# Four latent value blocks projected between the first head's scores, with weight preparation spread differently

## The chip, the cores and the metric

One core of a Trainium2 chip runs the whole program. It has a matrix engine (TensorE, "PE" in the profile, with its weight loads as "PEld"), a vector engine (VectorE, DVE), a scalar engine (ScalarE, ACT), a general engine (GpSimd, POOL) and a queue engine that issues transfers (SyncE, SP). Each engine runs its own instructions in its own order, and semaphores hold an instruction until what it needs is there. The metric is device time of one execution in microseconds (us). Times inside an execution come from one profiled execution and count from its span's start.

## The reference, cut to what matters

The program is one step of a two-layer diffusion backbone on 640 tokens: 512 latent tokens and 128 prompt tokens, width 1024. Layer 0 has two kinds of attention side by side, eight heads each, and one output projection over both:

```python
a_mla = attend_blocked(q, concat([k_lat, k_ctx]), concat([v_lat, v_ctx]), MLA_SCALE)   # 8 latent heads
a_na  = neighbourhood_attention(nq, nk, nv, c_nk, c_nv, rpb)                           # 8 neighbourhood heads
return concat([a_mla, a_na]) @ w_out
```

In the latent attention, keys and values are expanded from a 256-wide compressed latent: `kv = ckv @ w_ukv`, for 512 latent tokens, 128 cached tokens and 128 prompt tokens. The change lies where the neighbourhood heads end and the latent heads begin. Layer 1 has grouped-query attention, and every layer ends in a SwiGLU feed-forward network ("FFN"). Before each sub-layer a modulation (shift, scale, gate) is worked out from the conditioning: `silu(cond) @ w_mod + b_mod`.

## The kernel before, in words

**Precision.** A matrix operand is kept as two parts, a high part (a rounded copy) and a low part (the rest), and a product is three matmuls: high by high, high by low, low by high (`mm3`). So every operand costs one copy by ACT and one subtraction by DVE or POOL. `unit` (L168) does this for a slab of weights: load into a raw buffer, high part on ACT (L173), low part on DVE or POOL (L174). `rsplit` (L472) does it for a finished 128x640 activation, `pt_split` (L395, rows L401 and L402) for a transposed block of probabilities, and `vsplit` (L467, rows L469 and L470) for a projected block of values. Slabs sit in a ring of three raw buffers and a ring of three weight buffers, so that a slab can only be prepared once an older one is no longer read.

**Neighbourhood heads, then latent heads.** The loop over `h` from 0 to 7 in the first stage runs neighbourhood heads (names begin with n: `ns` scores, `np` probabilities, `nt` their transposes, `nts` the split transposes, `no` the head's output, `npp3` the prompt pair of heads 6 and 7). While head 7 runs, the keys (`mk`, `kT`) and queries (`mq`) of latent head 0 are projected too, from weights `wm0`; `mla_w(p)` makes `wm0` to `wm3`, the key and query weights of latent head pairs, and `wmv` holds the weights of the values. The next stage has latent heads 0 to 7 (names begin with m: `ms` scores, `mn` row maximum, `mp` probabilities from ACT at L992, `mr` the reciprocal sums, `mt` transposes, `mts` split transposes, `mo` the output). Each latent head has four score pieces s0 to s3, two query pieces q0 and q1 for the next head, and, of the head before, transposes and value products.

**Values.** The values of all latent heads are six blocks `mv0` to `mv5` of 128 tokens each; one block is six matmuls of 128x512. In the kernel before, mv0 and mv1 are projected (`mv_early`) among the last neighbourhood head's work and left in two banks of the matrix engine's result memory (PSUM), of the kind "y". After that stage is closed, `k_set` prepares keys of the odd heads (`kTo`, `kTq`), `vsplit` takes mv0 and mv1 out of their banks, and `open_y(s=2)` replaces the four "y" banks by two pairs of kind "s". The score pieces alternate between these two pairs, so the first score piece of latent head 0 writes where mv0 and mv1 lay. Blocks mv2 to mv5 are projected behind that by `mv_late`, in banks of another kind ("m"), one after the other, ahead of the first score.

**Order.** The order of pieces on TensorE is written out: `sequence(order, pieces)` runs the pieces by name, each bound behind the last matmul of the one before (`issue_after`). `MLA_ORDER[0]` and `MLA_ORDER[1]` are the orders of even and odd latent heads, and names of pieces that a head does not have are skipped. On the other engines a scheduler in the framework sets the order, so that a small edit can move rows there. `after(inst, fn)` holds work back until a named instruction has been placed, and `exps[h, j]` is the exponential of piece j of latent head h.

**Side work of the FFN.** While the FFN of layer 0 runs, DVE works out modulation columns of layer 1 from tiles of weights (`wm`, rows `junk`, two of 1.22 us for a tile). `mod_side` gets a plan with a number of tiles for each step of the FFN: steps "fb" over blocks of the hidden width, then steps "n" over the output blocks.

Of the kernel before, what the change touches and what calls it, by code (L numbers as in the profile page):

```python
# [14 lines left out]
ALU = mybir.AluOpType  # L15
# [36 lines left out]
def body(ctx, tc, xT, vecs, crow, wm0, wm0g1, wm0g, wm1, wA, wNV, wNA, wMK, wMV, wOA, wGQ, wGK, wGV, wOC,  # L52
# [112 lines left out]
        nc.sync.dma_start(raw[:, :n], src)  # L165
        return raw[:, :n]

    def unit(src, n, name, lo="v", pool=None, bufs=3):  # L168

        raw = load(src, n, name + "r")  # L170
        t = (pool or wp).tile([P, 2, 1024], F32R, tag="w", bufs=bufs, name=name)
        hi, lw = t[:, 0, :n], t[:, 1, :n]
        S.activation(hi, raw, AF.Copy)  # L173
        (V if lo == "v" else G).tensor_tensor(lw, raw, f(hi), ALU.subtract)  # L174
        return hi, lw

# [292 lines left out]
        S.activation(dst[:, :, 0:64], s3, AF.Copy)  # L469
        V.tensor_tensor(dst[:, :, 64:128], s3, f(dst[:, :, 0:64]), ALU.subtract)  # L470

    def rsplit(src, name):  # L472
        h = ring.tile([P, T], F32R, tag="hh", name=name + "h")
        l = ring.tile([P, T], F32R, tag="hl", name=name + "l")
        S.activation(h, src, AF.Copy)
        V.tensor_tensor(l, src, f(h), ALU.subtract)
# [350 lines left out]

    def mla_w(p):
        if p not in wmk:
            wmk[p] = unit(wMK[p], 768, f"wm{p}", lo="g")  # L830
        return wmk[p]

    def latents():
# [72 lines left out]
    for h in range(8):  # L906
        p, r = divmod(h, 2)
        if r == 0:
            oN.append(ring.tile([P, T], F32, tag="x", name=f"oN{p}"))
            pfirst, psecond = prompt_pair([nv[4][:, 2 * p + i, :] for i in range(2)], oN[p], ab, f"npp{p}",  # L910
                                         lambda name: bank(name, "y"))
        pts = []
        sc = na_scores(h, bm, pts)
        if h < 7:
            bm = na_bias(h + 1)
        qh, ql, ks = [t[r] for t in nqk[p]]
        pieces = named("s", sc)

        def prompt_scores(pss, qh=qh, ql=ql, ks=ks):
            PE.matmul(pss, qh[:, NS:T], ks[:, 896:1024], start=True, stop=False)  # L920
            PE.matmul(pss, ql[:, NS:T], ks[:, 896:1024], start=False, stop=True)
        pieces["sp"] = pfirst(r, prompt_scores)
        if p < 3:
            pieces.update(named("q", na_q(p + 1) if r == 0 else na_k(p + 1)))
        for n, at in enumerate(M_AT):
            if h == at:
                pieces.update(named("n" if "m0" in pieces else "m", mod0(4 + n, lambda n=n: bank(f"mod{4 + n}", "y"),
                                                                               mod_raw_w if h == 6 else mod_raw)))
        if h == 7:
            pieces.update(k_pieces(0, ybank))  # L930
            pieces.update(named("u", q_pieces(0, ybank, lambda c: ring.tile([P, T], F32R, tag="h" + c, name=f"mq{c}0"),
                                              lazy(lambda: load(tabM[:, 0, :], T, "tq0")))))
        sequence(NA_ORDER[h] if h else "q0 q1 s0 m0 q2 s1 sp q3 q4 q5 m1 q6 q7 m2", {**pieces, **tail})
        tail = na_values(h, pts, oN[p])
        if r == 1:
            tail.update(psecond)
        if h == 6:
            lat = latents()
            kT = [[ring.tile([P, T], F32R, tag="h" + c, name=f"kT{c}{r}") for r in range(2)] for c in "hl"]
            kTp = ring.tile([P, T], F32R, tag="x", name="kTp")  # L940
            even_keys, first_odd = [[(kT[i][r], kTp[:, P * (2 * i + r):P * (2 * i + r + 1)]) for i in range(2)] for r in range(2)]
            odd_keys = [first_odd]
            cqs = [rsplit(cq[u], f"cqs{u}") for u in range(2)]
            mla_w(0)
            wmv = unit(wMV, 1024, "wmv")
        if h == 7:
            for r in range(2):
                k_set(r, (slice(64, 128), slice(0, 64))[r], (0, 1, 2), kr)
# [75 lines left out]

    def mv_late(i):
        vsplit(mv[i], mv_of(i, bank))
    BESIDE = ()
    for i in range(6):
        if i not in mvb and i not in BESIDE:
            mv_late(i)  # L1030
# [5 lines left out]
    for h in range(8):  # L1036
# [22 lines left out]
        if r == 1:  # L1059
            tail.update(psecond)  # L1060
        if h in (0, 2, 4):
            oNs.append(after(exps[h, 3], lambda: rsplit(oN[len(oNs)], f"oNs{len(oNs)}")))
    oNs.append(after(exps[7, 2], lambda: rsplit(oN[3], "oNs3")))
    oMs = [after(exps[7, 3], lambda: rsplit(oM[p], f"oMs{p}")) for p in range(3)]
    sequence("w3 t0 y3 w4 t1 y4 t2 v0 t3 l0 pt v1 t4 l1 v2 v3 l2 v4 l3 l4 pv", {**tail, **late})
# [638 lines left out]
    def x_again(n):  # L1704
# [5 lines left out]
    op = ffn_open(0)  # L1710
    box, nxt = next_mod("h01", gs[0][1], mods[0], SH2, op[7])
    side, before = mod_side([(0, wm0g, G2)] + [(1, wm1[j:j + 8], j) for j in (SH1, SC1, G1, SH2, SC2)],
                            lambda kind, i: int(i > 4 and i % 3 > 0 or i == 21) if kind == "fb" else
                            (0, 1, 1, 1, 2, 2, 2, 2, 3, 3, 3, 3, 3, 2, 2, 2)[i])
    x, pend = mixer_out(wOA, oMs + oNs, [4, 5, 6, 7, 0, 1, 2, 3], x_again, mods[0], "oa", nxt, op[-1], before(op[1], op[5], (1, 1, 1, 1, 0, 0, 0)), True)
    box2, nxt = next_mod("h10", gs[1][0], mods[1], SH1)
    x, pend = ffn(0, x, pend, box["m"], nxt, side, op)
# [379 lines left out]
```

## Time and profile before

| what | value |
|---|---|
| time, median of three runs | 1475.41 us (1473.70 to 1478.78) |
| the profiled execution | 1473.37 us, span 1471.5 us, mean granted clock of TensorE 0.997 |
| PE busy | 1439.2 us (98%) |
| DVE busy | 1235.1 us (84%) |
| ACT busy | 783.9 us (53%) |
| POOL busy | 173.9 us (12%) |
| chain that ended last, by engine | PE 86%, DVE 6%, ACT 4% |

How to read it: the profiled execution is 2.04 us faster than the median of the runs, and 1.87 us of its time lie outside its span. PE's busy share is an average; what a change in one stage is worth shows in that stage's own idle time. A row of the timeline has its start, its duration, the engine, the line, the operation, what it writes and reads, the shape, how many instructions it groups, and in square brackets the idle time ahead of it with the instruction that ended it. A row of a window has, for each engine, the busy time and count of instructions in that stretch, then TensorE's granted clock, the share of the transfer engines and GB/s.

### The profile page before, as it was taken

To read this page: it belongs to the slowest core of one execution; us is meant where nothing else is said; L and a number is where in the kernel's file an instruction comes from. 1 tells how busy PE (TensorE), PEld (TensorE's weight loads), DVE (VectorE), ACT (ScalarE), POOL (GpSimd) and SP (SyncE) were. 2 spreads that over 40 slices of the span, in tenths; PEclk is the share of its full clock that TensorE was granted. 3 is DMA by queue.
4 is the path that set the end of the run, shared out by engine and by line. 5 is a ranking of instruction groups with operands and counts; after the bars stand their busy time and mean duration, and the time that the engine had idled before them with its cause. 6 is when DMAs were issued, how large, how long until landed. Compare 5 with 4: busy or idle time off the path is not lost.

```text
span 1471.5 us, 25831 instructions
## 1 busy us (share of the span) xinstructions
PE 1439.2 (98%) x9764; PEld 1388.8 (94%) x9764; DVE 1235.1 (84%) x2391; ACT 783.9 (53%) x1539; POOL 173.9 (12%) x270
## 2 busy tenths in 40 slices
PE   5999999999999999999999999999999999999997
PEld 3989978889999999999999999989999999999997
DVE  5877798877998888965997888888899898989976
ACT  5446687763755555531223656672656555555443
POOL 0046645420000000000000122220000000000000
PEclk9999999999999999999999999999999999999999
DMA  9653431025165555569764310115245555548572
GB/s 372 212 161 125 145 115 44 15 89 184 48 213 165 169 168 170 181 233 321 235 223 150 97 33 30 45 44 185 87 167 187 179 177 182 177 143 296 184 270 72
DMA packets 79636, 231.48 MB, mean 157 GB/s; under 512 B 8856, under 2 KB 13240, under 8 KB 79128
## 3 DMA queue, kind: packets, MB, share of 16 engines
q1 hardware_dynamic: 77152, 225.43, 45.7%
q10 hardware_dynamic: 1944, 3.48, 0.7%
q8 instruction: 76, 1.25, 0.3%
q0 software_dynamic: 416, 0.93, 0.2%
q14 instruction: 48, 0.39, 0.1%
HBM read 193.15 MB, written 36.66 MB: 156 GB/s over the span
## 4 chain that ended last, share of the span: by engine, by line
PE 86%; DVE 6%; ACT 4%; issue 2%; DMA 2%; POOL 1%; DVEq 0%; ACTq 0%; POOLq 0%
PE fg L64 21%; PE fd L64 9%; PE fgo L64 5%; PE fo L64 5%; PE fu L64 4%; PE gq L64 3%; PE fdo L64 2%; PE gs L64 2%; PE go L64 2%; PE fuo L64 1%; PE nq L64 1%; PE gt L68 1%; PE nk L64 1%; PE gvp L64 1%; PE mod L64 1%
## 5 line engine op out<-in xcount | busy, mean ns | idle before, releaser
L1664 DVE SCALAR_TENSOR_TENSOR junk<-wm,cb 128x1024 bf16<-128x1024 f32 x88 | 107.2, 1218 | 6.4 <-DMA wm<-in_wm 5.5
L64 PE MATMUL gq<-h10h,wgq 128*128 128x320 f32 x256 | 65.8, 316 | 0.0
L267 POOL TENSOR_SCALAR h10h<-h10t,gs,mods 128x320 fp32r<-128x320 f32 x4 | 3.9, 990 | 429.4 <-DVE h10t L261 427.1
L1404 ACT ACTIVATE wY<-s 128x1024 fp32r<-128x1024 f32 x38 | 40.3, 1061 | 25.4 <-PE fg L64 21.4
L1932 POOL TENSOR_TENSOR xr<-xw,fn1rs 128x320 f32<-128x320 f32 x2 | 1.7, 862 | 412.8 <-ACT fn1rs L235 412.8
L1404 ACT ACTIVATE wZ<-s 128x1024 fp32r<-128x1024 f32 x38 | 40.1, 1056 | 16.0 <-PE fd L64 11.7
L1405 DVE TENSOR_TENSOR wZ<-s,wZ 128x1024 fp32r<-128x1024 f32 x38 | 46.3, 1219 | 1.6
L1405 DVE TENSOR_TENSOR wY<-s,wY 128x1024 fp32r<-128x1024 f32 x38 | 46.3, 1219 | 0.3
L64 PEld LDWEIGHTS gq<-h10h,wgq 128*128 128x128 f32 x256 | 44.9, 189 | 0.6
L1513 DVE TENSOR_TENSOR sg<-up,sg 128x640 f32<-128x640 f32 x38 | 31.2, 822 | 15.8 <-ACT sg L1512 15.0
L1512 ACT ACTIVATE sg<-fg 128x320 f32<-128x320 f32 x38 | 16.7, 438 | 48.4 <-PE fg L64 48.4
L1534 ACT ACTIVATE p<-fd 128x320 f32<-128x320 f32 x38 | 16.6, 438 | 44.1 <-PE fd L64 44.1
L64 PE MATMUL gq<-h10l,wgq 128*128 128x320 f32 x128 | 39.4, 308 | 0.0
L1869 ACT ACTIVATE gp<-gs,gb,rq 128x640 f32<-128x640 f32 (+1 forms) x40 | 31.8, 796 | 13.2 <-DVE gb L1868 11.8
L64 PE MATMUL fg<-h01E,wW 128*128 128x320 f32 x228 | 36.6, 309 | 0.5 <-DVE g L1544 0.5
L64 PE MATMUL fg<-h11N,wZ 128*128 128x320 f32 x228 | 36.7, 309 | 0.0
L64 PE MATMUL fg<-h01q,wX 128*128 128x320 f32 x228 | 36.7, 309 | 0.0
L64 PE MATMUL fu<-h11q,wX 128*128 128x320 f32 x228 | 36.6, 309 | 0.0
L64 PE MATMUL fd<-h11q,wZ 128*128 128x320 f32 x228 | 36.6, 309 | 0.0
L64 PE MATMUL fd<-h01q,wZ 128*128 128x320 f32 x228 | 36.5, 309 | 0.0
L64 PE MATMUL fg<-h01C,wY 128*128 128x320 f32 x228 | 36.5, 309 | 0.0
L64 PE MATMUL fg<-h11q,wX 128*128 128x320 f32 x228 | 36.5, 309 | 0.0
(3421 smaller groups left out, 5299.4 us busy)
## 6 DMA issues: line engine op xcount, KB each, us to landing
wm<-in_wm SPq DMA_DIRECT2D x48, 512.0 KB, 4.2
mraw<-in_wm SPq DMA_DIRECT2D x8, 1024.0 KB, 13.1
mraw<-in_wm SPq DMA_DIRECT2D x14, 512.0 KB, 4.1
wmv<-in_wm0g SPq DMA_DIRECT2D x8, 512.0 KB, 4.1
wm<-in_wm0g SPq DMA_DIRECT2D x8, 512.0 KB, 5.1
ruo<-in_wFO SPq DMA_DIRECT2D x8, 512.0 KB, 3.9
rgo<-in_wFO SPq DMA_DIRECT2D x8, 512.0 KB, 5.3
x<-in_xT SPq DMA_DIRECT2D x8, 320.0 KB, 5.4
```

What stands on the lines that cost most here:

```text
L64: cls.last = nc.tensor.matmul(*a, **k)
L68: cls.last = nc.tensor.transpose(*a, **k)
L267: G.tensor_scalar(h[:, c0:c1], t, self.gsl[:, k, 0:1], self.ml[:, self.sh + k, 0:1], ALU.mult, ALU.add)
L1404: S.activation(h, src, AF.Copy)
L1405: V.tensor_tensor(w_, src, f(h), ALU.subtract)
L1512: last = S.activation(sg[:, 0:HT], g[:, :HT], AF.Silu, scale=-1.0)
L1513: V.tensor_tensor(sg, up, sg, ALU.mult)
L1534: S.activation(p5, b5[:, :HT], AF.Copy)
L1664: V.scalar_tensor_tensor(junk, raw, 1.0, cb[:, c, :], ALU.mult, ALU.mult, accum_out=mods[l][:, j0 + i, c:c + 1])
L1869: gexp[h, j] = S.activation(dst, src, AF.Exp, bias=nb, scale=rq[:, j:j + 1], accum_out=ll[:, j:j + 1])
L1932: G.tensor_tensor(x[k][:, c0:c1], root[1][k], nrm.rs[:, c0:c1], ALU.mult)
```

## The change

There are five edits.

1. The high part of the value weights `wmv` is made by POOL (`hi_by=G`), no longer by ACT.
2. `mla_w(p)` for p = 1, 2, 3 is held until the exponential of piece 1 of latent head 2p-2: `wm1` is prepared in head 0, `wm2` in head 2 and `wm3` in head 4. Before, all three were prepared as soon as a buffer was free.
3. Value blocks 2 to 5 are not projected ahead of the first score but inside latent head 0, whose order is now written out as s0 q0 s1 b2 q1 b3 s2 b4 s3 b5 (b2 is block 2).
4. The split of the finished neighbourhood outputs (`oNs0` to `oNs2`, in latent heads 0, 2 and 4) is done in two halves of 320 columns.
5. In the side plan of layer 0's FFN, one tile goes from "fb" step 20 to "n" step 0.

```diff
-    def unit(src, n, name, lo="v", pool=None, bufs=3):
+    def unit(src, n, name, lo="v", pool=None, bufs=3, hi_by=None):
...
-        S.activation(hi, raw, AF.Copy)
+        if hi_by:
+            hi_by.tensor_scalar(hi, raw, 1.0, 0.0, ALU.mult, ALU.add)
+        else:
+            S.activation(hi, raw, AF.Copy)
...
-    def rsplit(src, name):
+    def rsplit(src, name, parts=((0, T),)):
         h = ring.tile([P, T], F32R, tag="hh", name=name + "h")
         l = ring.tile([P, T], F32R, tag="hl", name=name + "l")
-        S.activation(h, src, AF.Copy)
-        V.tensor_tensor(l, src, f(h), ALU.subtract)
+        for c0, c1 in parts:
+            S.activation(h[:, c0:c1], src[:, c0:c1], AF.Copy)
+            V.tensor_tensor(l[:, c0:c1], src[:, c0:c1], f(h[:, c0:c1]), ALU.subtract)
         return h, l
...
-            wmk[p] = unit(wMK[p], 768, f"wm{p}", lo="g")
+            wmk[p] = after(exps.get((2 * p - 2, 1)), lambda: unit(wMK[p], 768, f"wm{p}", lo="g"))
...
-            wmv = unit(wMV, 1024, "wmv")
+            wmv = unit(wMV, 1024, "wmv", hi_by=G)
...
-    BESIDE = ()
+    BESIDE = 2, 3, 4, 5
...
-        sequence(MLA_ORDER[r], {**pieces, **late, **{k: v for k, v in tail.items() if k not in ("v3", "v4", "l3", "l4")}})
+        sequence(MLA_ORDER[r] if h else "s0 q0 s1 b2 q1 b3 s2 b4 s3 b5", {**pieces, **late, **{k: v for k, v in tail.items() if k not in ("v3", "v4", "l3", "l4")}})
...
-            oNs.append(after(exps[h, 3], lambda: rsplit(oN[len(oNs)], f"oNs{len(oNs)}")))
+            oNs.append(after(exps[h, 3], lambda: rsplit(oN[len(oNs)], f"oNs{len(oNs)}", HALF)))
...
-                            lambda kind, i: int(i > 4 and i % 3 > 0 or i == 21) if kind == "fb" else
-                            (0, 1, 1, 1, 2, 2, 2, 2, 3, 3, 3, 3, 3, 2, 2, 2)[i])
+                            lambda kind, i: int(4 < i < 20 and i % 3 > 0 or i == 21) if kind == "fb" else
+                            (1, 1, 1, 1, 2, 2, 2, 2, 3, 3, 3, 3, 3, 2, 2, 2)[i])
```

**TensorE, from the last neighbourhood work to the first latent score.** `npp3o` is the last product of the neighbourhood heads, `mv5` the last value block, `ms0_0` the first score piece and `mq10` the first query piece. Before, 16 rows (24 matmuls) of mv2 to mv5 follow `npp3o`; the last four of them and what follows:

```order
L64 MATMUL mv5_2858<-wmv_2560,ckph_2524 128x512 x2
L64 MATMUL mv5_2858<-wmv_2560,ckpl_2525 128x512
L64 MATMUL mv5_2858<-wmv_2560,ckph_2524 128x512 x2
L64 MATMUL mv5_2858<-wmv_2560,ckpl_2525 128x512
L64 MATMUL ms0_0_2872<-kTh0_2540,mqh0_2565 128x320 x2
L64 MATMUL ms0_0_2872<-kTl0_2542,mqh0_2565 128x320 x2
L64 MATMUL ms0_0_2872<-kTh0_2540,mql0_2566 128x320 x2
L64 MATMUL mq10_2886<-cqs0h_2545,wm0_2555 128x320
```

With the change:

```order
L64 MATMUL npp3o_2792<-npp3pth_2757,nv4_775 128x128
L64 MATMUL npp3o_2792<-npp3ptl_2758,nv4_775 128x128
L64 MATMUL ms0_0_2836<-kTh0_2540,mqh0_2565 128x320 x2
L64 MATMUL ms0_0_2836<-kTl0_2542,mqh0_2565 128x320 x2
L64 MATMUL ms0_0_2836<-kTh0_2540,mql0_2566 128x320 x2
L64 MATMUL mq10_2850<-cqs0h_2545,wm0_2555 128x320
```

The first score now stands directly behind `npp3o`; the 24 matmuls of mv2 to mv5 stand between the later pieces of head 0.

**DVE, the same stretch.** `oN3` takes the last neighbourhood outputs, `kTol` and `kTql` are odd keys, `mv` the value blocks, `mn0_0` the maximum of the first score piece. Before:

```order
L462 TENSOR_TENSOR oN3_2366<-npp3o_2792,npp3h_2797 64x128 x2
L867 TENSOR_TENSOR kTol_2815<-kr_587,kToh_2813 64x512
L867 TENSOR_TENSOR kTol_2815<-kr_587,kToh_2813 64x128
L867 TENSOR_TENSOR kTql_2816<-kr_587,kTqh_2814 64x128
L470 TENSOR_TENSOR mv0_2807<-mv0_2761,mv0_2807 128x8x64
L470 TENSOR_TENSOR mv1_2808<-mv1_2768,mv1_2808 128x8x64
L470 TENSOR_TENSOR mv2_2809<-mv2_2831,mv2_2809 128x8x64
L470 TENSOR_TENSOR mv3_2810<-mv3_2840,mv3_2810 128x8x64
```

With the change:

```order
L465 TENSOR_TENSOR oN3_2366<-npp3o_2792,npp3h_2797 64x128 x2
L871 TENSOR_TENSOR kTol_2815<-kr_587,kToh_2813 64x512
L871 TENSOR_TENSOR kTol_2815<-kr_587,kToh_2813 64x128
L871 TENSOR_TENSOR kTql_2816<-kr_587,kTqh_2814 64x128
L473 TENSOR_TENSOR mv0_2807<-mv0_2761,mv0_2807 128x8x64
L473 TENSOR_TENSOR mv1_2808<-mv1_2768,mv1_2808 128x8x64
L994 TENSOR_REDUCE mn0_0_2843<-ms0_0_2836 128x1
L893 TENSOR_TENSOR mqt10_2857<-mq10_2850,tq_2805 128x320
```

Up to mv1's low part the order is the same. The first score piece waits for that row in both programs, because it writes the banks that mv1 is read from.

**ACT, latent head 4.** `mts3_1h` to `mts3_4h` are split transposes of head 3, `mp4_2` a probability piece of head 4, `oaw0` and `oaw1` weights of the output projection. Before:

```order
L401 ACTIVATE mts3_1h_3560<-mt3_1_3555 128x512
L440 ACTIVATE mpp2p_3490,mpp2l0_3576<-ms4_2_3564,mpp2m0_3574 128x128
L401 ACTIVATE mts3_2h_3595<-mt3_2_3590 128x512
L173 ACTIVATE oaw1_4305<-oaw1r_4303 128x1024
L992 ACTIVATE mp4_2_3583,ml4_3491<-ms4_2_3564,mn4_2_3581 128x640
L890 ACTIVATE mqh5_3492<-mqt51_3607 128x320
L401 ACTIVATE mts3_3h_3617<-mt3_3_3612 128x512
```

With the change:

```order
L404 ACTIVATE mts3_1h_3564<-mt3_1_3559 128x512
L176 ACTIVATE wm3_3686<-wm3r_3684 128x768
L443 ACTIVATE mpp2p_3494,mpp2l0_3580<-ms4_2_3568,mpp2m0_3578 128x128
L404 ACTIVATE mts3_2h_3599<-mt3_2_3594 128x512
L176 ACTIVATE oaw0_4264<-oaw0r_4262 128x1024
L996 ACTIVATE mp4_2_3587,ml4_3495<-ms4_2_3568,mn4_2_3585 128x640
L894 ACTIVATE mqh5_3496<-mqt51_3611 128x320
L404 ACTIVATE mts3_3h_3621<-mt3_3_3616 128x512
L176 ACTIVATE oaw1_4311<-oaw1r_4309 128x1024
```

`wm3` and `oaw0` now stand in head 4 ahead of `oaw1`. Before, `wm3` stood in head 0 and `oaw0` in head 2. On DVE the low parts of `oaw0` and `oaw1` move in the same way.

## The prediction

> **What bounds the kernel now.** The page's busy shares come first, then TensorE's (PE) list of waits.
>
> ```profile
> PE 1439.2 (98%) x9764; PEld 1388.8 (94%) x9764; DVE 1235.1 (84%) x2391; ACT 783.9 (53%) x1539; POOL 173.9 (12%) x270
> ```
>
> ```profile
> PE ms L64 <- ACT mp L992: 2.6, 4, 1.0
> PE mo L64 <- DVE mts_0l L402: 1.1, 2, 0.9
> ```
>
> PE sets the time, and an edit is worth what it does to PE's idle time. The windows over the changed stage (PE first, with its busy time and count, then PEld, DVE, ACT, POOL, the granted clock) show where idle time is left:
>
> ```profile
> 200.00:225.00 25.00, 21.94 (x131) 19.11 (x130) 22.09 (x59) 18.69 (x46) 8.36 (x10) 1.00 0.25 79
> 225.00:250.00 25.00, 23.94 (x161) 21.91 (x160) 19.82 (x46) 20.04 (x48) 15.52 (x19) 1.00 0.14 44
> 250.00:275.00 25.00, 24.75 (x163) 22.11 (x162) 22.86 (x49) 20.20 (x49) 10.85 (x14) 1.00 0.07 22
> 275.00:300.00 25.00, 23.84 (x157) 21.31 (x156) 22.14 (x48) 19.55 (x47) 10.76 (x14) 1.00 0.07 22
> 300.00:325.00 25.00, 23.63 (x152) 20.46 (x152) 20.62 (x39) 17.45 (x37) 7.79 (x8) 1.00 0.19 64
> 600.00:625.00 25.00, 25.00 (x173) 25.00 (x172) 23.65 (x37) 13.19 (x21) 0.00 (x0) 1.00 0.59 185
> ```
>
> From 200 to 325 PE is idle for 3.06 + 1.06 + 0.25 + 1.16 + 1.37 = 6.90 us: all that this stage can give. In the FFN (last row) it is never idle. PE's timeline has the places:
>
> ```profile
> 203.39 0.50 PE L64 MATMUL no<-nts_0l,nv 128*128 128x512 f32 x1 [1.61 <-DVE nts_0l L402]
> 205.35 0.39 PE L64 MATMUL mk<-ckph,wm 128*128 128x256 f32 x1 [0.86 <-DVE nm L784]
> 215.59 0.28 PE L64 MATMUL npp3o<-npp3ptl,nv 128*128 128x128 f32 x1
> 215.70 0.67 PE L64 MATMUL mv<-wmv,ckh 128*128 128x512 f32 x2
> 221.23 0.45 PE L64 MATMUL ms<-kTh,mqh 128*128 128x320 f32 x2
> 224.51 0.56 PE L64 MATMUL ms<-kTh,mqh 128*128 128x320 f32 x2 [0.49 <-ACT mp L992]
> 228.71 0.56 PE L64 MATMUL ms<-kTh,mqh 128*128 128x320 f32 x2 [0.97 <-ACT mp L992]
> 278.77 0.56 PE L64 MATMUL ms<-kTh,mqh 128*128 128x320 f32 x2 [0.16 <-ACT mp L992]
> 285.08 0.49 PE L64 MATMUL mo<-mts_0h,mv 128*128 128x512 f32 x1 [0.89 <-DVE mts_0l L402]
> ```
>
> **Edit 1 and wm1's hold: upstream gain, -0.75.** ACT loses two operations:
>
> ```profile
> 197.47 1.05 ACT L173 ACTIVATE wmv<-wmvr 128x1024 fp32r<-128x1024 f32 x1
> 199.62 0.85 ACT L173 ACTIVATE wm<-wm1r 128x768 fp32r<-128x768 f32 x1
> ```
>
> Both stand ahead of the split behind which PE idles 1.61 and 0.86, so the bounds are 0 and -2.47. DVE is nearly full there and holds most of it back:
>
> ```profile
> 198.07 0.48 DVE L386 SCALAR_TENSOR_TENSOR gs<-mods,vec 128x16 f32<-128x16 f32 x1
> 201.74 0.75 DVE L413 TENSOR_TENSOR oN<-no,nhs 64x448 f32<-64x448 f32 x2 [0.40 <-ACT nhs L411]
> ```
>
> The 0.40 that DVE waits for ACT goes, and the gs row (0.48) moves behind this stretch: 0.88 at most, of which I take 0.75. POOL's new 128x1024 copy is not in the trace; its copy of 128x384 takes 0.59, so it costs no less than that, no more than 0.59 x 1024/384 = 1.6, and some 1.1 if a part of the 0.59 is a fixed start. It stands ahead of np6_3, which the transposes need:
>
> ```profile
> 197.95 0.59 POOL L393 TENSOR_SCALAR np<-np,nr_3r 128x384 f32<-128x384 f32 x1 [0.30 <-DVE npp3r0r L392]
> 198.39 1.04 PE L68 MATMUL nt<-ident,np 128*128 128x128 f32 x8
> ```
>
> np6_3 was there 0.15 us after these transposes (of 128x384 blocks in turn) began, and comes about 1.1 - 0.3 = 0.8 later. So PE stands still there, by up to 0.8, and then less at 203.39, where it waits 1.61 for DVE in any case: this moves idle time and adds none, unless DVE's chain from the transposes on has no slack; then the 0.75 is lost. Bounds for the whole step: +0.1 and -2.47.
>
> **Edit 3: a wait uncovered, +2.8.** The first score piece writes the banks in which mv0 and mv1 lay, so it waits for DVE's low part of mv1, second of the six in the last row here. Columns as in the rows above, ACT and DVE in order of time:
>
> ```profile
> 215.51 0.59 ACT L411 ACTIVATE nhs<-no 64x512 f32<-64x512 f32 x1 [0.99 <-PE no L64]
> 216.13 0.75 DVE L413 TENSOR_TENSOR oN<-no,nhs 64x448 f32<-64x448 f32 x2 [1.16 <-ACT nhs L411]
> 217.00 0.38 ACT L460 ACTIVATE npp3h<-npp3o 64x256 f32<-64x256 f32 x1 [0.90 <-DVE oN L413]
> 217.41 0.58 DVE L462 TENSOR_TENSOR oN<-npp3o,npp3h 64x128 f32<-64x128 f32 x2 [0.53 <-ACT npp3h L460]
> 218.02 0.89 DVE L867 TENSOR_TENSOR kTol<-kr,kToh 64x512 fp32r<-64x512 f32 x2
> 218.84 0.28 DVE L867 TENSOR_TENSOR kTql<-kr,kTqh 64x128 fp32r<-64x128 f32 x1
> 219.04 3.71 DVE L470 TENSOR_TENSOR mv<-mv,mv 128x512 fp32r<-128x512 f32 x6
> ```
>
> mv1 is out at 219.04 + 2 x 3.71/6 = 220.3. PE is done with npp3o at 215.87. Before, mv2 to mv5 filled 215.70 to 221.23 (5.53 us), and the wait cost nothing. With the change PE has nothing to do from 215.87 to 220.3: 4.4 us. The chain hangs on PE's own last products, so an earlier start upstream shifts both ends and shortens nothing. The 24 matmuls are done later instead, and two gaps in head 0 that they cover go (0.49 and 0.97). 4.4 - 1.46 = 2.97; each idle time hides about 0.17 of the last matmul's drain (its 0.28 against a step of 0.11), two go and one comes, which leaves 2.8. Bounds: 0 if score banks came free earlier than the rows say, 4.4 if the two gaps come back.
>
> **Is the clock lost as well? +1.2.** The granted clock falls to one half in two places only:
>
> ```profile
> 19.57:22.98 3.41, 1.75 (x24) 1.08 (x28) 2.17 (x6) 2.23 (x4) 0.00 (x0) 1.00 1.03 412
> 22.98:26.40 3.42, 3.42 (x23) 2.23 (x18) 3.42 (x11) 2.01 (x6) 0.00 (x0) 0.50 1.03 410
> 200.48:203.89 3.41, 1.80 (x10) 1.23 (x9) 2.98 (x10) 3.35 (x8) 1.83 (x1) 1.00 0.55 145
> 1463.41:1466.82 3.41, 0.11 (x2) 0.00 (x0) 3.41 (x8) 1.35 (x3) 1.68 (x2) 1.00 0.81 290
> 1466.82:1470.00 3.18, 0.00 (x0) 0.00 (x0) 0.69 (x2) 0.00 (x0) 0.00 (x0) 0.50 0.97 352
> ```
>
> It fell at 22.98 after 3.41 us in which PE was busy for 1.75, with small products (128*32), came back at 26.40, and fell again at 1466.82 after 0.11 of 3.41; 1443.84 us lie between, 423 times 3.413. So the clock goes by a fixed beat of 3.41 us. A beat with 1.80 us of large products (third row) was no reason to lower it. An idle time of 4.4 fills at least 2.2 of some beat, which leaves PE 1.2 of 3.41 or less: between the cases, and nearer, I think, to those that lost the clock (6 in 10). The price is half of what a lowered beat covers of PE's work behind the idle time: 0.7 to 2.2 by where the beat falls, mostly 1.5; 0.3 of it comes back where PE would have waited for ACT anyway.
>
> [...]
>
> **Edit 2: later heads, 0.** wm2 and wm3 leave head 0 (ACT 2 x 0.85, POOL 2 x 1.83), which shortens small gaps of heads 1 to 3: of the 1.31 idle from 225 to 275, 0.97 is counted already, so -0.3 at most, and -0.2 with oaw0 gone from head 2; I take -0.5. Head 4 pays:
>
> ```profile
> 273.07 1.06 ACT L173 ACTIVATE oaw<-oaw1r 128x1024 fp32r<-128x1024 f32 x1
> 274.44 1.22 DVE L174 TENSOR_TENSOR oaw<-oaw1r,oaw 128x1024 fp32r<-128x1024 f32 x1
> ```
>
> A second such pair (oaw0) and wm3's 0.85 on ACT come right beside it. DVE is late by 1.22, and the score piece at 278.77, which waits already, with it. Behind it the 0.89 at 285.08 goes, since DVE catches up in its own gaps. 1.22 - 0.89 = 0.33, with ACT's share +0.5; bounds 0 and 1.22 + 0.85 = 2.07.
>
> **Edits 4 and 5: 0.** Two halves cost DVE some 2 x 0.48 for the 0.81 of one (0.15 more, three times), and start earlier; rows:
>
> ```profile
> 223.40 0.48 DVE L889 TENSOR_TENSOR mqt<-mq,tq 128x320 f32<-128x320 f32 x1
> 231.18 0.81 DVE L476 TENSOR_TENSOR oNs0l<-oN,oNs0h 128x640 fp32r<-128x640 f32 x1
> ```
>
> The moved FFN tile is DVE work (1.35 us in 25 idle) beside a PE without a gap; without that cover it costs its own two rows, 2.4.
>
> **The sum.** -0.75 + 2.8 + 1.2 - 0.5 + 0.5 = +3.25 on the profiled execution's 1473.37: 1476.6. The median of the runs lies 2.04 above it (1475.41), so 1478.7, rounded to 1478.5.
>
> **Rivals.**
> - *The clock stays up*: 1477.5, chance 0.27. The row of 200.48 speaks for it, with 53% busy at full clock.
> - *The filled gaps win*: all 6.90 us of PE's idle time go, since ACT and POOL are relieved from 195 to 270, and 4.4 come: -2.5, so 1472.9; without a new wait 1470. For it: the waits are on ACT's probabilities and DVE's splits. Against: DVE, which holds most of them, loses only a row of 0.48. Chance 0.15.
> - *Head 4 takes the loss in full, slower*: wm3, oaw0 and oaw1 in one head, at DVE 22.14 of 25 and ACT 19.55. If DVE does not catch up by 282, PE pays 2.07 there and the 0.89 stays: 3.25 + 2.07 - 0.5 = 4.8, with no gain in heads 1 to 3 5.3: 1480.5. It decides once ms5_1 starts later than 280. Chance 0.1.
> - *Nothing shows*: the idle time moves and stays as long, 1475.4 +- 0.7. Chance 0.05.
>
> **How the numbers follow.** The forecast has the rest, 0.43. 0.3%, about what a measurement of this kernel tells from no change, is 4.4 us: 1471.0 and 1479.8. Slower: a quarter of the forecast's own spread (+-1.5), the head 4 case and a little of the second, 0.22. Faster: a third of the filled gaps, 0.06. Same: 0.72. Range 1473 to 1482; the forecast's own is 1476.5 to 1480.5.
>
> **What would show it.** Right: PE idle for about 4.4 us ahead of the first score, ended by DVE at L473; the clock at 0.50 in the 3.4 us around 220 to 225; no wait above 0.3 inside head 0; PE's gaps between 198 and 206 together near 1.7. Wrong: a first score within 1 us of npp3o, or a gap behind it shared out to later pieces. Waits of over 1 us at ms5_1 would say that head 4 pays in full.

## The result, and the profile after

The changed kernel takes 1482.56 us (median of seven runs, 1480.23 to 1484.84) against 1473.70 us of the kernel before in seven runs (1472.71 to 1478.78). The ratio is 1.0049, 95% interval 1.0034 to 1.0064: slower. The forecast of 1478.5 stood 3.1 us above the 1475.41 that it set out from; the ratio makes 0.0049 x 1473.70 = 7.2 us, more than twice as much. The changed kernel's median lies 0.56 us above the upper end of the range, 1482. (The two medians are 8.86 us apart, a ratio of 1.0060, inside the same interval.)

TensorE's list of waits of the changed kernel (engine, line, what released it: total us, times, longest) already names three places:

```profile
PE ms L64 <- DVE mv L473: 4.6, 1, 4.6
PE ms L64 <- ACT mp L996: 3.7, 3, 2.4
PE nt L68 <- POOL np L396: 1.2, 1, 1.2
PE mo L64 <- DVE mts_0l L405: 0.5, 2, 0.3
```

Before, the first of these did not exist, and the second was 2.6 in four parts of at most 1.0. TensorE's timeline of the changed kernel gives the times:

```profile
199.41 0.76 PE L68 MATMUL nt<-ident,np 128*128 128x128 f32 x5 [1.20 <-POOL np L396]
...
214.42 0.28 PE L64 MATMUL npp3o<-npp3ptl,nv 128*128 128x128 f32 x1
219.29 0.87 PE L64 MATMUL ms<-kTh,mqh 128*128 128x320 f32 x2 [4.59 <-DVE mv L473]
...
231.83 0.47 PE L64 MATMUL ms<-kTh,mqh 128*128 128x320 f32 x2
...
283.59 0.85 PE L64 MATMUL ms<-kTh,mqh 128*128 128x320 f32 x2 [2.36 <-ACT mp L996]
```

The first score piece waits 4.59 us for DVE's low part of mv1, the row that the prediction named. The gaps inside head 0 are gone. The row at 231.83 is the first score of head 1 (228.71 before). At 283.59, a score piece that waited 0.16 before waits 2.36. It is piece 1 of head 5 (ms5_1), and it writes the banks that the exponential of head 4's last piece reads, so it stands still when head 4's work on DVE and ACT is late; in what follows this is the wait in head 4. Both rows behind a wait take 0.85 or more for two matmuls that take 0.56 elsewhere. The windows around the two waits show why (behind POOL's column come the granted clock, the share of the transfer engines and GB/s):

```profile
215.41:218.82 3.41, 0.00 (x0) 0.00 (x0) 2.84 (x9) 2.38 (x6) 0.00 (x0) 1.00 0.00 0
218.82:222.23 3.41, 2.94 (x11) 2.97 (x12) 1.15 (x2) 0.04 (x1) 0.00 (x0) 0.50 0.00 0
280.26:283.67 3.41, 1.05 (x6) 0.57 (x5) 3.38 (x6) 1.30 (x3) 0.00 (x0) 1.00 0.71 207
283.67:287.09 3.42, 3.42 (x11) 3.03 (x12) 2.06 (x6) 1.84 (x4) 2.15 (x3) 0.50 0.25 102
```

The granted clock is at one half for 3.41 us behind each of the two, and full elsewhere in this stage. The two beats begin at 218.82 and 283.67: 64.85 us apart, 19 times 3.413.

To see where time goes, one compares the start of the same matmul in both traces. Each entry is the start in the changed kernel minus that in the kernel before, in us:

| matmul | difference | what lies between |
|---|---|---|
| first npp2o (195.98 before) | -0.86 | ahead of the change, by chance: from -0.95 to +1.30 in the other profiles |
| last npp3o (215.59) | -1.17 | upstream: -0.31 |
| first score of head 1 (228.71) | +3.12 | first score and head 0: +4.29 |
| first score of head 5 (276.00) | +2.54 | scores of heads 1 to 4 ("heads 1 to 3" in the prediction): -0.58 |
| last score of head 5 (287.08) | +5.76 | scores of head 5, with the wait in head 4: +3.22 |
| last score of head 7 (308.20) | +5.77 | 0 |
| gate product fg<-h01E of the FFN (653.96) | +8.53 | output projection and FFN of layer 0: +2.76 |

The attention stage alone loses -0.31 + 4.29 - 0.58 + 3.22 = 6.62 us, and the ratio gives 7.2. So what was lost up to the last matmul of the table (for short, the FFN's loss) in this one execution has to be tested; experiments do that.

### The profile page after: what moved, and what is told of

It reads as the page before. It is cut to its first block, busy times and chain, and to the rows that moved or that the text cites. A ratio compares the mean times of both kernels' runs of the same rounds, so it can differ in the third digit from the quotient of the medians.

```text
span 1480.5 us, 25836 instructions
## 1 busy us (share of the span) xinstructions
PE 1440.3 (97%) x9764; PEld 1390.6 (94%) x9764; DVE 1237.4 (84%) x2394; ACT 783.3 (53%) x1541; POOL 175.2 (12%) x271
## 4 chain that ended last, share of the span: by engine, by line
PE 78%; DVE 11%; DMA 4%; ACT 4%; issue 2%; DVEq 0%; POOL 0%; ACTq 0%; SPq 0%
PE fg L64 16%; PE fd L64 7%; PE fgo L64 5%; PE fo L64 5%; PE fu L64 4%; PE gq L64 3%; PE fdo L64 2%; PE gs L64 2%; PE go L64 2%; PE nk L64 2%; PE fuo L64 1%; PE ms L64 1%; PE nq L64 1%; PE gt L68 1%; DVE junk L1668 1%
## 5 line engine op out<-in xcount | busy, mean ns | idle before, releaser
L64 PE MATMUL fg<-h01N,wZ 128*128 128x320 f32 x228 | 36.6, 309 | 0.4 <-ACT p L1536 0.4
```

Of the source, the lines that this page charges most:

```text
L64: cls.last = nc.tensor.matmul(*a, **k)
```

## The experiments

Theory A: three places lose time by themselves: the uncovered wait of the first score (edit 3), the crowded head 4 (edit 2), and perhaps the side plan (edit 5); the clock falls behind the first two. The rivals are in the expectations. One table has the results; "head 0" is the difference to before that arises from the last npp3o to the first score of head 1, "heads 4, 5" the same from the first to the last score of head 5, both in the one profiled execution; "clock" says whether it fell behind the wait, for one beat of 3.41 us or for two; "hidden" means that value blocks cover the wait.

| run | ratio to before (95%) | wait of first score | clock | head 0 | wait in head 4 | clock | heads 4, 5 |
|---|---|---|---|---|---|---|---|
| changed kernel | 1.0049 (1.0034 to 1.0064) | 4.59 | fell | +4.29 | 2.36 | fell | +3.22 |
| side plan back | 1.0035 (1.0022 to 1.0047) | 4.59 | fell, two beats | +5.17 | 2.37 | fell | +2.32 |
| blocks back | 1.0009 (1.0000 to 1.0018) | hidden | stayed | +0.14 | 2.36 | fell | +3.22 |
| hold back | 1.0019 (1.0009 to 1.0028) | 4.59 | fell, two beats | +5.38 | 0.17 | stayed | -0.57 |
| two blocks ahead | 1.0016 (1.0007 to 1.0026) | 1.79 | stayed | +1.36 | 2.38 | stayed | +1.70 |
| changed kernel again | 1.0040 (1.0026 to 1.0055) | 4.59 | fell | +4.43 | 2.37 | fell | +3.06 |
| side plan only | 1.0002 (0.9992 to 1.0012) | hidden | stayed | +0.01 | 0.16 | stayed | +0.01 |
| hold only | 1.0013 (1.0004 to 1.0023) | hidden | stayed | +0.14 | 2.36 | stayed | +1.61 |
| one block beside | 1.0003 (0.9994 to 1.0013) | none | stayed | -0.39 | 0.17 | stayed | -0.57 |
| two blocks, split first | 0.9988 (0.9977 to 0.9999) | 0.80 | stayed | -0.53 | 0.15 | stayed | -0.50 |
| changed, split first | 1.0037 (1.0021 to 1.0054) | 3.61 | fell | +3.35 | 2.36 | fell | +3.16 |
| POOL's high part only | 0.9994 (0.9984 to 1.0004) | hidden | stayed | +0.01 | 0.17 | stayed | -0.01 |

**Side plan back.** The changed kernel with edit 5 undone:

```diff
-                            lambda kind, i: int(4 < i < 20 and i % 3 > 0 or i == 21) if kind == "fb" else
-                            (1, 1, 1, 1, 2, 2, 2, 2, 3, 3, 3, 3, 3, 2, 2, 2)[i])
+                            lambda kind, i: int(i > 4 and i % 3 > 0 or i == 21) if kind == "fb" else
+                            (0, 1, 1, 1, 2, 2, 2, 2, 3, 3, 3, 3, 3, 2, 2, 2)[i])
```

> The changed kernel with the old side plan of the first feed-forward network (edit 5 undone). Theory A (the loss has three separate places: the first latent score, latent head 4, and the side plan): TensorE's idle time between 400 and 660, 2.5 us in the changed kernel (0.36 + 0.62 + 0.11 and a wait of 1.39 for DVE's row g), falls back to the 0.55 of before, and the time by about 2.8 us, to 1.003 of before; head 0 and head 4 keep their waits of 4.6 and 2.4. Theory B (the feed-forward network only inherits a lateness of DVE and ACT from the attention): the 2.5 us stay, and the ratio stays at 1.005.

The ratio is 1.0035, its interval overlapping that of the changed kernel. The FFN lost 1.07 us against before, not 2.76. That fits neither theory well; the runs below with the new plan bear on it.

**Blocks back.** The changed kernel with edit 3 undone:

```diff
-    BESIDE = 2, 3, 4, 5
+    BESIDE = ()
...
-        sequence(MLA_ORDER[r] if h else "s0 q0 s1 b2 q1 b3 s2 b4 s3 b5", ...
+        sequence(MLA_ORDER[r], ...
```

> The changed kernel with the four value blocks ahead of the first score again (edit 3 undone). Theory A: the wait of 4.6 us ahead of the first score and the fall of the clock there go; head 1 starts about 4 us earlier against the same point upstream, the wait in head 4 (2.4) stays, ratio about 1.002. Theory C (the late value blocks also push head 4, since DVE and ACT carry their splits into later heads): the wait in head 4 goes too, and the ratio is 1.000.

The ratio is 1.0009. TensorE's waits there:

```profile
223.27 0.57 PE L64 MATMUL ms<-kTh,mqh 128*128 128x320 f32 x2 [0.49 <-ACT mp L996]
227.60 0.56 PE L64 MATMUL ms<-kTh,mqh 128*128 128x320 f32 x2 [1.09 <-ACT mp L996]
279.53 0.90 PE L64 MATMUL ms<-kTh,mqh 128*128 128x320 f32 x2 [2.36 <-ACT mp L996]
```

No wait at the first score, and the two gaps of head 0 are back (before: 0.49 and 0.97); head 0 costs 4.15 us less than in the changed kernel. Head 4 waits 2.36 all the same. Theory A stands: head 4 does not hang on the blocks.

**Hold back.** The changed kernel with edit 2 undone:

```diff
-            wmk[p] = after(exps.get((2 * p - 2, 1)), lambda: unit(wMK[p], 768, f"wm{p}", lo="g"))
+            wmk[p] = unit(wMK[p], 768, f"wm{p}", lo="g")
```

> The changed kernel with the pair weights prepared as early as before (edit 2 undone). Theory A: the wait of 2.4 us in head 4 (piece 1 of head 5) falls to 0.2 to 0.5, the clock does not fall there, and about 3.2 us go: ratio 1.0025 to 1.003; the wait of 4.6 us at the first score stays. Rival D (the wait in head 4 comes from the split in halves or from the value blocks): it stays above 2 us, and the ratio at 1.005.

The ratio is 1.0019. This is the other half: the first score waits, head 4 does not.

```profile
221.67 0.87 PE L64 MATMUL ms<-kTh,mqh 128*128 128x320 f32 x2 [4.59 <-DVE mv L473]
284.49 0.56 PE L64 MATMUL ms<-kTh,mqh 128*128 128x320 f32 x2 [0.17 <-ACT mp L996]
```

Head 0 costs +5.38 here, and +5.17 with the side plan back, with the same wait as in the changed kernel (+4.29). In these two executions the clock stood at one half for two beats. The beats here:

```profile
216.78:220.19 3.41, 0.29 (x3) 0.15 (x2) 2.27 (x7) 2.49 (x7) 0.00 (x0) 1.00 0.02 6
220.19:223.61 3.42, 1.94 (x7) 1.97 (x8) 1.33 (x3) 0.43 (x1) 0.00 (x0) 0.50 0.00 0
223.61:227.02 3.41, 3.41 (x13) 3.32 (x13) 1.56 (x4) 1.35 (x3) 1.12 (x2) 0.50 0.00 0
```

The first beat had 0.29 us of work and lowered the clock. In the second, work began only at 221.67, and the clock stayed down for the third too. In the changed kernel the query products (128x320) follow one another every 0.27 us in the beat at half clock (from 221.03) and every 0.15 us behind it (from 224.72), nearly twice as fast. So as an estimate, half of 1.94 + 3.41, 2.7 us, is lost to the clock here; in the changed kernel's one beat it is half of 2.94, 1.47.

Beyond the expectation, head 5 gains 0.57 us: the wait that was 0.89 at 285.08 before is 0.33 here. DVE's low part of oNs2 stands in the chain ahead of it, whole before and in halves here:

```profile
282.59 1.25 DVE L476 TENSOR_TENSOR oNs2l<-oN,oNs2h 128x640 fp32r<-128x640 f32 x1 [0.39 <-ACT oNs2h L475]
```

```profile
288.05 0.90 DVE L480 TENSOR_TENSOR oNs2l<-oN,oNs2h 128x320 fp32r<-128x320 f32 x2
```

The two halves together take 0.35 less than the whole row, and the wait of 0.39 for ACT's high part is gone. That edit 4 does this is argued from these rows; no run has edit 4 alone.

**Two blocks ahead.** The changed kernel with mv2 and mv3 ahead of the first score:

```diff
-    BESIDE = 2, 3, 4, 5
+    BESIDE = 4, 5
...
-"s0 q0 s1 b2 q1 b3 s2 b4 s3 b5"
+"s0 q0 s1 q1 b4 s2 b5 s3"
```

> The changed kernel with blocks 2 and 3 ahead of the first score, and blocks 4 and 5 in head 0 (order s0 q0 s1 q1 b4 s2 b5 s3). Theory A: the two blocks cover 2.8 us of the wait, so 1.6 to 1.8 us of it are left, and the granted clock stays at 1.00 through head 0, because the beat of 3.41 us then has TensorE busy for at least half of it. Head 1 starts 2.5 to 4 us earlier against the same point upstream; ratio about 1.0025. If the clock falls for an idle time of 1.7 us as well, some 1.2 us less is gained, and the clock shows 0.50 for 3.4 us.

The ratio is 1.0016. Two blocks take 4.59 - 1.79 = 2.80 us out of the wait, and the clock stays at 1.00 through head 0. Head 0 costs +1.36 instead of +4.29. Its two waits account for that: 1.79 and 1.01 here, less the 0.49 and 0.97 of before, make 1.34. The second is a gap that blocks 2 and 3 no longer fill:

```profile
221.19 0.53 PE L64 MATMUL ms<-kTh,mqh 128*128 128x320 f32 x2 [1.79 <-DVE mv L473]
230.80 0.56 PE L64 MATMUL ms<-kTh,mqh 128*128 128x320 f32 x2 [1.01 <-ACT mp L996]
```

In head 4, the same wait as in the changed kernel (2.38) is there, and the clock stays up. TensorE's row and the two beats around it:

```profile
283.04 0.56 PE L64 MATMUL ms<-kTh,mqh 128*128 128x320 f32 x2 [2.38 <-ACT mp L996]
```

```profile
278.29:281.71 3.42, 2.38 (x15) 1.88 (x13) 3.14 (x5) 1.78 (x3) 1.38 (x2) 1.00 0.81 272
281.71:285.12 3.41, 2.08 (x11) 1.92 (x12) 3.04 (x7) 2.54 (x6) 1.16 (x2) 1.00 0.53 160
```

The border between the two, 281.71, falls into the wait here, and neither beat has TensorE busy for less than 2.08 us. (Where the clock does not change, the place of a border is the author's estimate, in steps of 3.413 us.) In the changed kernel one beat held the whole wait and had 1.05. Head 4 costs 1.70 in this run and 3.22 in that one: the same wait, without the clock's fall and with it.

**The changed kernel again**, with no edit, for a second profile.

> The changed kernel once more, unaltered, for a second profile. In the first profile the feed-forward network of layer 0 lost 2.8 us against before (TensorE idle at 420, 470 to 500 and 662). If edit 5 or the later start of the attention's end causes it, it comes again: 2 us or more. If it is scatter of single executions (when weight transfers land), which the three runs with the new side plan and a loss of 0.2 or less speak for, it is under 1 us now. The wait of 4.59 at the first score and of 2.36 in head 4 come again to 0.05 us; the clock falls at both or, by the place of the beat, at the first alone.

The ratio is 1.0040. Both waits come again to 0.01 us, and the clock falls at both. The FFN lost 0.74 us instead of 2.76; TensorE's wait at the gate product fg<-h01E, in the first and in the second profile:

```profile
662.49 1.74 PE L64 MATMUL fg<-h01E,wW 128*128 128x320 f32 x10 [1.39 <-DVE g L1548]
```

```profile
660.68 2.03 PE L64 MATMUL fg<-h01E,wW 128*128 128x320 f32 x12 [0.92 <-DVE g L1548]
```

So 2 of those 2.76 us belong to one execution.

**Side plan only**, the kernel before with edit 5 alone:

```diff
-                            lambda kind, i: int(i > 4 and i % 3 > 0 or i == 21) if kind == "fb" else
-                            (0, 1, 1, 1, 2, 2, 2, 2, 3, 3, 3, 3, 3, 2, 2, 2)[i])
+                            lambda kind, i: int(4 < i < 20 and i % 3 > 0 or i == 21) if kind == "fb" else
+                            (1, 1, 1, 1, 2, 2, 2, 2, 3, 3, 3, 3, 3, 2, 2, 2)[i])
```

> The kernel before with edit 5 alone (the moved tile of the side plan). Theory: no change, ratio 0.9995 to 1.0005, and TensorE's idle time between 400 and 660 within 0.5 us of before's 0.55. Rival: the plan costs 1.5 to 2.8 us, ratio 1.001 to 1.002.

The ratio is 1.0002: edit 5 costs nothing that these runs can tell. Its profile has 1.7 us of loss in the FFN, but the kernel before with POOL's high part alone, which leaves the plan as it was, has 1.75 there, and three runs with the new plan have 0.14 to 0.24. The loss does not follow the plan, it scatters; by what, no run here isolates. This profile shows something else. The stage ahead of the latent heads is untouched in it, and yet the clock falls there:

```profile
201.65:205.07 3.42, 1.40 (x9) 1.19 (x10) 3.29 (x12) 3.40 (x10) 1.33 (x3) 1.00 0.38 115
205.07:208.48 3.41, 3.41 (x17) 3.41 (x17) 2.93 (x12) 2.37 (x11) 0.82 (x2) 0.50 0.00 0
```

The gaps that the kernel before has at 203 and 205 (1.61 and 0.86) are 1.74 and 0.86 in this execution, and 2.02 us of the two fall into one beat. In the profile of before they lie in two, with the border at 203.89 (26.40 and 52 times 3.413, an estimate), and the clock stayed. From npp2o to mv0 this execution lost 1.39 us by it.

**Hold only**, the kernel before with edit 2 alone:

```diff
-            wmk[p] = unit(wMK[p], 768, f"wm{p}", lo="g")
+            wmk[p] = after(exps.get((2 * p - 2, 1)), lambda: unit(wMK[p], 768, f"wm{p}", lo="g"))
```

> The kernel before with edit 2 alone (pair weights held back). Theory: head 4 pays by itself: piece 1 of head 5 waits 2.4 us instead of 0.16, and the clock falls there if the beat lies so; the first score's wait stays hidden. Ratio 1.0015 to 1.0025. Rival: the wait needs the value blocks or the halves beside it; then it stays under 1 us and the ratio at 1.000.

The ratio is 1.0013. Head 4 pays by itself:

```profile
280.93 0.56 PE L64 MATMUL ms<-kTh,mqh 128*128 128x320 f32 x2 [2.36 <-ACT mp L992]
```

The clock stayed up. By the same estimate a border, 279.18, falls into the wait; of the two beats, this one has less work:

```profile
279.18:282.59 3.41, 1.66 (x9) 1.55 (x10) 3.04 (x6) 2.13 (x6) 0.81 (x1) 1.00 0.56 204
```

Upstream this run gained 0.57 us, more than the 0.31 of the changed kernel: wm1 out of the way helps, and POOL's high part takes a part of that back.

**One block beside.** The changed kernel with three blocks ahead of the first score, wm1 alone held back, the old side plan, and:

```diff
-            wmk[p] = after(exps.get((2 * p - 2, 1)), lambda: unit(wMK[p], 768, f"wm{p}", lo="g"))
+            wmk[p] = after(exps.get((0, 1)) if p == 1 else None, lambda: unit(wMK[p], 768, f"wm{p}", lo="g"))
...
-    k_set(1, slice(0, 64), (0, 1, 2), kr, 1)
     for i, pss in mvb.items():
         vsplit(mv[i], pss)
+    k_set(1, slice(0, 64), (0, 1, 2), kr, 1)
...
-    BESIDE = 2, 3, 4, 5
+    BESIDE = 5,
...
-"s0 q0 s1 b2 q1 b3 s2 b4 s3 b5"
+"s0 q0 s1 s2 b5 q1 s3"
```

> What the runs so far leave standing: POOL's high part, the halves, wm1 alone held back (to head 0), the old side plan, blocks 2 to 4 ahead of the first score and block 5 alone in head 0 (s0 q0 s1 s2 b5 q1 s3), and the splits of blocks 0 and 1 ahead of the odd keys. Theory: the first score waits under 0.5 us since three blocks (4.1 us) cover the chain; head 1 starts 0.8 to 1.2 us earlier than before against the same point upstream, head 5 another 0.6 by the halves, 0.3 upstream: 1.7 to 2.1 us in all, ratio 0.9985 to 0.9990. Rival: the gaps only move behind block 5 and into head 1, ratio 0.9995 to 1.0005.

The ratio is 1.0003: no difference, so the rival was right about the time, and only in part about the reason. The first score no longer waits, and head 0 gains 0.39. But wm1, held to head 0, pushes wm2 and wm3 behind it, and head 1 loses 3.8 us. TensorE's waits there, and POOL's rows:

```profile
235.54 0.77 PE L68 MATMUL mt<-ident,mp 128*128 128x128 f32 x5 [1.54 <-POOL mp L396]
239.32 0.50 PE L64 MATMUL mo<-mts_0h,mv 128*128 128x512 f32 x1 [1.25 <-DVE mts_0l L405]
```

```profile
227.02 1.86 POOL L177 TENSOR_TENSOR wm<-wm1r,wm 128x768 fp32r<-128x768 f32 x1
...
229.96 1.86 POOL L177 TENSOR_TENSOR wm<-wm2r,wm 128x768 fp32r<-128x768 f32 x1
...
232.58 1.85 POOL L177 TENSOR_TENSOR wm<-wm3r,wm 128x768 fp32r<-128x768 f32 x1
234.38 1.10 POOL L396 TENSOR_SCALAR mp<-mp,mr_3r 128x640 f32<-128x640 f32 x1
```

Three low parts stand on POOL ahead of the scaling of head 0's last probabilities, for which the transposes wait.

**Two blocks, split first.** This run therefore holds one slab to each head. It is the kernel before with:

```diff
-            wmk[p] = unit(wMK[p], 768, f"wm{p}", lo="g")
+            wmk[p] = after(exps.get((p - 1, 1)), lambda: unit(wMK[p], 768, f"wm{p}", lo="g"))
...
-    k_set(1, slice(0, 64), (0, 1, 2), kr, 1)
     for i, pss in mvb.items():
         vsplit(mv[i], pss)
+    k_set(1, slice(0, 64), (0, 1, 2), kr, 1)
...
-    BESIDE = ()
+    BESIDE = 4, 5
...
-        sequence(MLA_ORDER[r], ...
+        sequence(MLA_ORDER[r] if h else "s0 q0 s1 b4 s2 b5 q1 s3", ...
...
-            oNs.append(after(exps[h, 3], lambda: rsplit(oN[len(oNs)], f"oNs{len(oNs)}")))
+            oNs.append(after(exps[h, 3], lambda: rsplit(oN[len(oNs)], f"oNs{len(oNs)}", HALF)))
```

> A version built on the kernel before: wm1, wm2 and wm3 held back to heads 0, 1 and 2 (one slab for a head), the halves, blocks 4 and 5 in head 0 (s0 q0 s1 b4 s2 b5 q1 s3), the splits of blocks 0 and 1 ahead of the odd keys, the high part of the value weights on ACT as before. Theory: 0.5 us upstream (as with the pair weights held alone), the first score waits under 1 us, head 1 starts 1.2 us earlier than before against the same point upstream, no wait over 0.3 in head 4, 0.6 in head 5 by the halves: 1.7 to 2.4 us, ratio 0.9984 to 0.9990. Rival: the gaps come back behind the blocks, ratio 0.9995 to 1.0005.

The ratio is 0.9988 (0.9977 to 0.9999): 1473.30 us against 1474.88 of the kernel before, run beside it. By the ratio it beats the kernel before by about 1.8 us, with an interval that ends just short of no difference. Its first score waits 0.80:

```profile
218.58 0.53 PE L64 MATMUL ms<-kTh,mqh 128*128 128x320 f32 x2 [0.80 <-DVE mv L470]
253.41 0.56 PE L64 MATMUL ms<-kToh,mqh 128*128 128x320 f32 x2 [0.54 <-ACT mp L993]
```

By its profile it gains 0.58 upstream, 0.53 in head 0 and 0.50 in heads 4 and 5, and loses 0.13 in between, where wm3 and oaw0 stand together in head 2 and piece 1 of head 3 waits for it (second row): 1.48 us in all.

**Changed kernel, split first.** Two statements exchanged, nothing else:

```diff
-    k_set(1, slice(0, 64), (0, 1, 2), kr, 1)
     for i, pss in mvb.items():
         vsplit(mv[i], pss)
+    k_set(1, slice(0, 64), (0, 1, 2), kr, 1)
```

> The changed kernel with the splits of value blocks 0 and 1 ahead of the odd keys (two statements exchanged). Theory: the wait at the first score is the chain on DVE up to mv1's low part; without kTol and kTql in it (0.89 + 0.28) it falls from 4.59 to 3.4 us. With that, the beat of 3.41 us has TensorE busy for 0 to 1.7 us: the clock falls there in most cases, and stays if the idle time is cut in two by the beat. Rival: the wait hangs on something else (ACT's high parts); then it stays at 4.6.

The ratio is 1.0037. The wait falls to 3.61, not 3.4. DVE's rows:

```profile
217.58 0.58 DVE L465 TENSOR_TENSOR oN<-npp3o,npp3h 64x128 f32<-64x128 f32 x2 [0.53 <-ACT npp3h L463]
218.20 1.29 DVE L473 TENSOR_TENSOR mv<-mv,mv 128x512 fp32r<-128x512 f32 x2
219.41 0.88 DVE L871 TENSOR_TENSOR kTol<-kr,kToh 64x512 fp32r<-64x512 f32 x2
```

So the wait is this chain, and kTol and kTql were 0.98 us of it. The expectation added up their rows, 0.89 and 0.28; but the rows overlap, and from the start of kTol at 216.86 to the start of mv's row at 217.87 the changed kernel has 1.01 us. The clock fell with 3.61 us as with 4.59.

**POOL's high part only**, the kernel before with edit 1 alone:

```diff
-            wmv = unit(wMV, 1024, "wmv")
+            wmv = unit(wMV, 1024, "wmv", hi_by=G)
```

> The kernel before with edit 1 alone (the high part of the value weights by POOL). Theory: POOL's copy takes 1.0 to 1.6 us, np6_3 comes later, and TensorE waits 1.2 us for it ahead of the transposes at 198; the waits at 203 and 205 shrink by as much, so from npp2o to npp3o the gain is 0 to 0.2 us. Rival: ACT's relief is worth 0.75 us there, as predicted.

The ratio is 0.9994, no difference within its interval; upstream it gains 0.31 us by the profile. POOL's, DVE's and TensorE's rows:

```profile
196.40 1.20 POOL L174 TENSOR_SCALAR wmv<-wmvr 128x1024 fp32r<-128x1024 f32 x1
197.58 0.73 POOL L396 TENSOR_SCALAR np<-np,nr_2r 128x384 f32<-128x384 f32 x1
198.29 1.54 POOL L396 TENSOR_SCALAR np<-np,nr_3r 128x384 f32<-128x384 f32 x1
```

```profile
197.94 1.45 DVE L177 TENSOR_TENSOR wmv<-wmvr,wmv 128x1024 fp32r<-128x1024 f32 x1
```

```profile
199.89 0.77 PE L68 MATMUL nt<-ident,np 128*128 128x128 f32 x5 [1.20 <-POOL np L396]
```

The copy costs 1.20. It also brings DVE's low part of the same weights (197.94 to 199.39) over POOL's np6_3, which takes 1.54 instead of 0.59. TensorE waits 1.20 for it. The waits at 203 and 205 (1.61 and 0.86 before) shrink to one of 0.82, so that little is left.

## Why the prediction was right or wrong, point by point

- **Upstream, predicted -0.75; measured -0.31.** The copy on POOL came out as estimated (1.20 for 1.1). The step that failed is "np6_3 comes about 0.8 later": measured from the first npp2o it began 0.73 later, and it took 0.95 longer besides, while DVE's subtraction ran. In the kernel before, the same subtraction ran beside POOL's npp3p, for which TensorE did not wait. The new wait of 1.20 was only in part taken from the waits behind it: 1.61 and 0.86 became 0 and 0.82.
- **The wait at the first score, predicted 4.4 and +2.8 net; measured 4.59, and +2.8 net.** Head 0 lost 4.29; the beat from 218.82 at half clock had TensorE busy for 2.94, of which half, 1.47, is the clock's (an estimate from this row). 4.29 - 1.47 = 2.82. Of the 4.59, 0.15 lies between the end of DVE's row at 219.14 and the start of the score. Undoing edit 3 took the wait away, exchanging two statements shortened it, and two blocks ahead cut it to 1.79: this cause is shown.
- **The clock, predicted +1.2 at 6 in 10, with bounds 0.7 and 2.2; it fell in all five executions with a wait of 3.6 or more there.** The price by the estimate above was 1.47 in the changed kernel, but 2.5 and 2.7 with the side plan back and with the hold back, where the clock stayed at one half for a second beat (with hold back, behind 1.94 us busy). The reasoning by beats held, the chance was too low: a wait of 4.59, however it falls across two beats, leaves one of them at most (6.83 - 4.59)/2 = 1.1 us of work, and the clock fell behind beats with 0 to 1.40 in these runs. What the prediction left out: the clock fell at another wait too, the 2.36 us in head 4.
- **Heads 1 to 3, predicted -0.5; measured -0.58.** The number came out partly by luck. The prediction took it from small gaps, but those listed in that stretch grew from 0.34 to 0.52 in all. The gain is made of steps of 0.05 to 0.16 us between single matmuls, which no list of waits shows.
- **Head 4, predicted +0.5 with bounds 0 and 2.07; measured +3.22, outside the bounds.** This is the main step that failed, and it makes up most of the 3.4 us that the forecast's 3.25 lacks to 6.62. The forecast let DVE be late by one oaw0 (1.22) and catch up. DVE's and ACT's rows of the changed kernel in head 4:

```profile
275.67 0.16 DVE L395 RECIPROCAL mpp2r0r<-mpp2l 128x1 f32<-128x1 f32 x1 [0.39 <-ACT mpp2p L443]
...
277.47 1.22 DVE L177 TENSOR_TENSOR oaw<-oaw0r,oaw 128x1024 fp32r<-128x1024 f32 x1
...
279.68 1.61 DVE L177 TENSOR_TENSOR oaw<-oaw1r,oaw 128x1024 fp32r<-128x1024 f32 x1 [0.26 <-ACT oaw L176]
...
281.80 0.82 DVE L994 TENSOR_REDUCE mn<-ms 128x1 f32<-128x640 f32 x1
```

```profile
274.45 0.84 ACT L176 ACTIVATE wm<-wm3r 128x768 fp32r<-128x768 f32 x1
...
278.56 1.09 ACT L176 ACTIVATE oaw<-oaw1r 128x1024 fp32r<-128x1024 f32 x1
```

  wm3 on ACT makes DVE wait 0.39, oaw0 costs 1.22, DVE waits 0.26 for oaw1's high part, and oaw1's low part takes 0.39 longer than before: 2.26 in all, and the row maximum at 281.80 (276.97 before, with 2.54 of earlier delay) is 2.29 late. Nothing lay between it and the score piece in which DVE could catch up: the gaps that the forecast counted on come behind that piece. The clock then takes 1.5 more (3.22 less the 1.70 of two blocks ahead). The wait of 0.89 behind it shrank to 0.30, as the forecast had it; hold only, without the halves, has 0.26 there, so this is not the halves' doing. That edit 2 alone makes the wait is shown by its two runs, both ways; what the clock adds is shown by two blocks ahead and hold only, where it stayed up and the stretch cost 1.70 and 1.61.
- **The halves, predicted 0; measured -0.5 to -0.6** where head 4 has no wait of its own (hold back, one block beside, and the run with two blocks and the split first). All three have other edits besides, so this rests on the rows shown with hold back. **The side plan, predicted 0; measured 1.0002.**
- **The rivals.** The case that came is the slower one, with head 4 paying in full; its condition, a start of ms5_1 later than 280, was met (278.77 + 2.28 = 281.05 against the same point ahead). Its chance of 0.1 was too small, and its price, which let the clock fall only once, too low. "The filled gaps win" is out: in head 0 the gaps were filled as hoped, and that cost three times what they held. (Its price without a new wait, 1470, does not follow from its terms: 1475.41 - 6.90 is 1468.5.) "The clock stays up" failed at both waits.

## What to carry to other kernels

Work that seems to stand in the way on the critical engine may be the cover of a wait that no list of waits shows; before moving it, find what the next instruction waits for and when that is done. Preparation that is held back has to be spread: each slab needs a stage in which every engine that it uses has room for it, and slabs that queue behind it in the same buffers move with it. When a wait of some microseconds on TensorE appears, count the clock with it, at each place where it appears: here the same wait of 2.36 to 2.38 us in head 4 cost 1.61 and 1.70 us where the clock stayed, and 2.32 to 3.22 us where it fell.

## What the runs showed of the hardware

- **The granted clock changed in steps of 3.413 us, whose place is not tied to the program.** Two falls lie 1443.84 us apart in the kernel before (423 steps) and 64.85 us in the changed kernel (19 steps). In the two profiles of the changed kernel the clock fell at 218.82 and at 219.35, 0.53 apart, while the first score moved by 0.19.
- **In the attention stage the clock fell behind four beats in which TensorE was busy for 0 to 1.40 us, and stayed behind three with 1.66 to 2.08.** Those of the fall are 0 and 1.05 (changed kernel), 0.29 (hold back) and 1.40 (side plan only), which is 41% of 3.41. The others are 1.66 (hold only), 1.80 (before) and 2.08 (two blocks ahead), with borders estimated as above. The same wait of 2.4 us in head 4 was followed by a fall in five profiles (changed kernel twice, side plan back, blocks back, changed with split first: scores of head 5 +2.32 to +3.22) and by none in two (two blocks ahead +1.70, hold only +1.61).
- **Busy time alone does not sort the beats of these runs.** In blocks back the clock also fell at 866.64, behind a beat with 2.92 us busy. Ten products of only two columns (`gr`, 1.17 us in the kernel before) lie in that beat; whether they count for less, no run isolates. The beat in blocks back:

```profile
863.22:866.64 3.42, 2.92 (x23) 2.47 (x21) 3.36 (x7) 1.88 (x6) 0.59 (x1) 1.00 0.35 101
866.64:870.05 3.41, 3.41 (x15) 3.37 (x14) 2.05 (x5) 2.19 (x5) 0.00 (x0) 0.50 0.13 53
```

- **Two of POOL's rows took longer beside DVE's subtraction of 128x1024.** np6_3 (128x384) took 1.54 us beside it with POOL's high part only, and 0.59 without in the kernel before. There, where the same subtraction ran at 198.56 for 1.23 us, it was npp3p (128x128) that took 1.43, against 0.37 with POOL's high part only. No run varies that subtraction, so what in it does this is not shown.
